# Issue order of norms, heads and weight pieces in a two-layer hybrid encoder

## The chip, the cores and the metric

The program runs on one core of a Trainium2 chip. The metric is the device time of one execution in microseconds (us), as the median of several runs. The profile is of one execution.

## The reference

Two layers of a macaron block run over one sequence of 256 tokens with 1024 channels, in float32. What matters here:

```python
def swiglu(h, w_gu, w_down):
    g, u = jnp.split(h @ w_gu, 2, axis=-1)
    return (jax.nn.silu(g) * u) @ w_down

for l in range(DEPTH):                      # DEPTH = 2, D_MODEL = 1024, D_FF = 2816
    x = x + 0.5 * swiglu(rmsnorm(x, g_ffn1[l]), w_ffn1_gu[l], w_ffn1_down[l])
    x = x + hybrid_mixer(rmsnorm(x, g_mix[l]), ...)
    x = x + 0.5 * swiglu(rmsnorm(x, g_ffn2[l]), w_ffn2_gu[l], w_ffn2_down[l])
return rmsnorm(x, g_final)
```

The mixer makes one input projection of `h` and splits its columns into three kinds of attention heads of width 64. Six forgetting heads add to the scores a running sum of log-sigmoid forget logits:

```python
c = jnp.cumsum(jax.nn.log_sigmoid(f_logit), axis=1)
bias = c[:, :, start:end, None] - c[:, :, None, :end]
p = jax.nn.softmax(jnp.where(mask, s + bias, -jnp.inf), axis=-1)
```

Five stick-breaking heads use a reversed cumulative sum of log(1 - sigmoid) in place of a softmax. Five sparse heads attend only to the 64 keys that an indexer scores highest for each query:

```python
rel = relu(einsum('bqhd,bkd->bqhk', iq, ik)); score = einsum('bqhk,bqh->bqk', rel, iw)
_, sel = lax.top_k(score, 64)
```

Each kind has its own up-projection (384, 320 and 320 rows) to 1024 channels, multiplied by a sigmoid gate (3 x 1024 gate columns of the input projection); the sum goes through one output projection.

## The kernel before

**Products.** Every weight is split into two float16 parts, `whi` and `wlo`, and the activations likewise; a projection adds three products (hi x hi, hi x lo, lo x hi) for each block of 128 rows. `project_T` (line 337) keeps the weight as the stationary operand and moves the 256 tokens; `project` (lines 372 to 374) does it the other way round.

**Weight pipeline.** All weights are cut into chunks, in the order in which they are used. `emit_raw` issues the DMA of a raw float32 part from SyncE into one of `RAW_BUFS` = 5 buffers. `emit_piece` turns a part into a piece, `whi` on ScalarE (line 249) and `wlo` on VectorE (line 251), in one of `HL_BUFS` = 6 buffer pairs. `advance(i)`, called when piece `i` is about to be used, issues pieces up to `i + HL_BUFS` and raw loads `RAW_BUFS` ahead of the last of them. Up-projections of 320 rows end in a block of 64 rows; it is loaded twice, to both halves of the partitions, is a piece of its own, and takes two products instead of three.

**Steps beside the projections.** Work that is not a projection lives in generators, the tasks. After every second block of 128 rows (every fourth where a chunk has 256 columns or less), `background()` takes one step of the first two tasks in the list. A `yield` ends a step. `finish()` takes all the remaining steps of a task at once. The tile framework then fixes an order for each engine: an instruction that is issued earlier has priority, and one that a planner's model of times holds not yet ready is passed by those behind it. On the chip each engine keeps that order.

**Norms.** `Norm.half` makes the split parts of the next activations and squares; the task `stats` then sums the squares by a product (`ss`, line 520), makes `rstd` (`power` on GpSimd), and on its last step spreads it over the partitions by a product (`rb`, line 546). `stats` has two empty steps, then `ss`, then an empty one, then `rb`. In `ffn`, `gate(k)` scales the first half of the gated unit by that result and applies SiLU; it is tried before every block of the `u` chunk, does nothing for `k < 4` while the result is missing, and from `k = 4` on takes the steps of the norm itself. `FirstNorm` does the same for the first norm of the program, from transposes of the input `x`; its squares run on ScalarE inside its `stats`.

**Mixer order.** Input groups 0 and 1 (indexer, sparse queries and latent), 2 and 3 (forgetting keys and queries), 4 (forgetting values and forget logits), 5 to 7 (stick-breaking), then six gate chunks. `indexer` is a task from group 1 on, `latent` from group 2 on, `forget` from group 5 on. `forget` makes `fr` from the logits in its first step; its second is the cumulative product `cps` (line 946) and then the operands `kb` and `qb`. The heads are tasks in pairs: three of `fox_heads`, three of `dsa_heads`, and, after group 7, three of `stick_heads`; the last of either five is a single head. A pair makes its operands, waits three steps, makes scores, and ends with `values`. The first step of `fox_heads` calls `t_f.finish()`. After the gate chunks every task left is finished at once; then come sigmoids, which are ordered behind all exponentials (line 1145), six up-projections and the output projection.

**Buffers that heads share.** PSUM tag `at` has two banks for scores and cumulative sums; tag `qT` has four buffers, one for a head's operand and two more for the split sums of a stick-breaking head; tag `mm` has four banks for projections.

Of the kernel before, what the change touches and what calls it, by code (L numbers as in the profile page):

```python
# [129 lines left out]
def trunk(ctx, tc, io, out, flag):  # L130
# [69 lines left out]
    RAW_BUFS, HL_BUFS = (4, 6) if wide else (5, 6)  # L200
    raws, pieces, chunk_pieces = [], [], []
    for ci, (nm, l, r, c, n) in enumerate(chunks):
        nk = -(-r // P)
        rk = 4 if n > 256 else 8
        pk = rk // 2 if wide else rk
        cuts = [0, 1, 2, 3, 4, 6, 8] if ci == 0 else [0, 2, 4, 6, 8] if ci == 1 else list(range(0, nk, rk)) + [nk]
        lst = []
        for k0, k1 in zip(cuts, cuts[1:]):
            ks = list(range(k0, k1))
            raws.append((ci, ks))  # L210
            full = [k for k in ks if (k + 1) * P <= r]
            for i in range(0, len(full), pk):
                sub = full[i:i + pk]
                lst.append(len(pieces))
                pieces.append((len(raws) - 1, sub[0] - k0, len(sub), P, sub))
            if len(full) < len(ks):
                k = ks[-1]
                lst.append(len(pieces))
                pieces.append((len(raws) - 1, k - k0, 1, r - k * P, [k]))
        chunk_pieces.append(lst)  # L220

# [4 lines left out]
    def emit_raw():  # L226
# [4 lines left out]
        t = wp.tile([P, RAW], F32, tag="raw", bufs=RAW_BUFS, name=f"raw{i}")  # L231
# [40 lines left out]
    def advance(i):  # L272

        while state["piece"] < min(state.get("hold", len(pieces)), i + HL_BUFS):
            emit_piece()
        last = pieces[state["piece"] - 1][0]
        while state["raw"] < min(len(raws), last + RAW_BUFS):
            emit_raw()


    class Task:
        def __init__(self, gen):
            self.gen, self.done, self.steps = gen, False, 0
            tasks.append(self)
# [20 lines left out]
    def background(n=2):  # L305
        for t in list(tasks[:n]):
            t.step()
# [7 lines left out]
    def project_T(nm, l, c, n, rhs, banks, ready=None):  # L315
# [8 lines left out]
        for pi in plist:  # L324
            advance(pi)
            wh, wl = hl_tiles[pi]
            half = pieces[pi][3] == HD
            for j, k in enumerate(pieces[pi][4]):
                if ready:
# [73 lines left out]
    nc.scalar.dma_start(grow0, io["g_ffn1"].rearrange("l (k p) -> (l k) p", p=P))  # L403
    for t in range(NT):
# [20 lines left out]
    warm_up(9)  # L425
# [53 lines left out]
    class Norm:  # L479
# [34 lines left out]
        def stats(self):  # L514
            yield
            yield
# [46 lines left out]
    class FirstNorm(Norm):  # L563


        def __init__(self, gcol, nm):
# [3 lines left out]
            self.copies, self.last = [], ()  # L570
# [19 lines left out]
        def begin(self, ks=range(4)):  # L590
# [6 lines left out]
            if k == 3:  # L597
                state["hold"] = state["piece"]
            else:
                self.task = Task(self.stats())  # L600

# [4 lines left out]
        def stats(self):  # L606
            self.ss = sp.tile([P, NT, 2], F32, tag="ss", name="ss" + self.nm)
            for h in range(2):
                for k, v in self.copies[2 * h:2 * h + 2]:
                    copy = behind(nc.scalar.copy(xT[:, k - 1:k + 1, :], v), self.last[0])  # L610
                yield
                for t in range(NT):
                    behind(square(x[:, t, h * 512:(h + 1) * 512], self.ss[:, t, h:h + 1], f"{self.nm}_{h}{t}"),
                           copy)
            yield
            ms = self.mean_square()
# [6 lines left out]
    def ffn(l, gu, dn, norm, nxt):  # L623
# [10 lines left out]
        for c, n in FF_CHUNKS:  # L634
# [5 lines left out]
            def gate(k):  # L640
                if s or (norm.R is None and k < 4):
# [121 lines left out]
    def mixer(l, norm, nxt):  # L763
# [101 lines left out]
        def indexer():  # L865
# [31 lines left out]
            for i in range(TOPK // 8):  # L897
# [4 lines left out]
                yield  # L902
            X["pen"] = sp.tile([P, 3 * P], BF16, tag="pen", name="pen" + L)
# [27 lines left out]
        def forget():  # L931
# [11 lines left out]
            yield  # L943
# [74 lines left out]
        def fox_heads(heads, nm):  # L1018
            t_f.finish()
# [4 lines left out]
            for _ in range(3):  # L1024
                yield
            kb, qb = X["kb"], X["qb"]
# [74 lines left out]
        t_idx = Task(indexer())  # L1101
        group(*IN_GROUPS[1], [(0, WC, True, PQC), (WC, P, False, PCKV)])
        t_lat = Task(latent())
# [6 lines left out]
        t_f = Task(forget())  # L1110

        for i, hs in enumerate(pairs(HA)):
            Task(later(fox_heads(hs, f"a{l}"), 2 * (i == 1)))
# [125 lines left out]
```

## Time and profile before

| | us |
|---|---|
| median of 3 runs | 1162.74 (1158.06 to 1163.47) |
| the profiled execution | 1166.04 |
| its span, first to last instruction | 1164.2 |
| TensorE busy in the span | 1126.7 |
| VectorE busy | 776.9 |
| ScalarE busy | 618.8 |
| DMA read from HBM | 207.35 MB |

The span is what the instructions take; 1.8 us of the profiled execution lie around it. Matmuls are pipelined, so a busy TensorE is not TensorE at its peak, and a stretch at half clock counts as busy too.

### The profile page before, as it was taken

The numbers are of one execution on the slowest core, as the hardware profiler recorded it, in microseconds if no ns is written. First come the engines' busy times: TensorE is split into PE (matmuls) and PEld (weight loads), VectorE is DVE, ScalarE is ACT, GpSimd is POOL, SyncE is SP. The second block draws the span as 40 slices with busy tenths as digits, with TensorE's granted clock in tenths as the row PEclk, the third lists the DMA queues.
The fourth block names the chain that finished last, engine by engine and source line by source line (L and its number), as shares of the span: only waits on it lengthen the run. The fifth ranks groups of instructions, "written<-read, shape, count | busy, mean of one in ns | idle before, by whom it ended". The sixth has DMA issues, their size and how long they took to land.

```text
span 1164.2 us, 22885 instructions
## 1 busy us (share of the span) xinstructions
PE 1126.7 (97%) x9752; PEld 964.2 (83%) x9752; DVE 776.9 (67%) x1357; ACT 618.8 (53%) x841; POOL 12.9 (1%) x25
## 2 busy tenths in 40 slices
PE   8999999989999999999999999999999999999997
PEld 7788887767888878888888888867788887888756
DVE  5865655897657966564576574579965789555642
ACT  6644544666657644353454363366575685544530
POOL 0000000000000000000000000000000000000000
PEclk9999999999999989999999999999999999999998
DMA  8956655455333866466665475556533249455711
GB/s 296 367 166 209 218 164 168 150 181 182 110 91 107 293 218 173 157 233 201 218 209 166 167 234 174 174 169 201 183 128 110 78 157 331 159 164 182 248 41 40
DMA packets 118770, 209.95 MB, mean 180 GB/s; under 512 B 4818, under 2 KB 43908, under 8 KB 118660
## 3 DMA queue, kind: packets, MB, share of 16 engines
q1 hardware_dynamic: 118340, 207.88, 54.9%
q8 instruction: 78, 1.28, 0.4%
q10 hardware_dynamic: 320, 0.53, 0.1%
q14 instruction: 32, 0.26, 0.1%
HBM read 207.35 MB, written 1.05 MB: 179 GB/s over the span
## 4 chain that ended last, share of the span: by engine, by line
PE 76%; DVE 13%; ACT 5%; issue 3%; DMA 1%; POOL 1%; POOLq 0%; DVEq 0%; ACTq 0%
PE uw_ffn_gu L337 19%; PE gw_ffn_gu L337 17%; PE d0w_ffn_down L337 7%; PE gt L337 7%; PE d512w_ffn_down L337 7%; DVE wlo L251 7%; PE in L337 3%; ACT whi L249 3%; PE up L337 1%; DMA raw<-in_w_ffn_gu_dram 1%; PE in L374 1%; PE in L372 1%; PE in L373 1%; DVE xTlof L493 1%; PE ya L974 1%
## 5 line engine op out<-in xcount | busy, mean ns | idle before, releaser
L251 DVE SCALAR_TENSOR_TENSOR wlo<-raw,whi 128x2048 f16<-128x2048 f32 (+7 forms) x232 | 452.7, 1954 | 268.4 <-ACT whi L249 267.7
L337 PEld LDWEIGHTS <-whi 128*128 128x128 f16 x5504 | 540.8, 99 | 69.9 <-issue 2.6
L249 ACT ACTIVATE whi<-raw 128x2048 f16<-128x2048 f32 (+7 forms) x232 | 379.2, 1640 | 400.6 <-issue 136.6
L337 PEld LDWEIGHTS <-wlo 128*128 128x128 f16 x2768 | 272.7, 99 | 37.5 <-issue 3.0
L337 PE MATMUL gw_ffn_gu<-xTlof,whi 128*128 128x256 f16 x704 | 194.1, 276 | 1.0 <-DVE xTlof L493 1.0
L337 PE MATMUL gw_ffn_gu<-xThif,wlo 128*128 128x256 f16 x704 | 193.9, 276 | 0.8 <-DVE wlo L251 0.8
L337 PE MATMUL gw_ffn_gu<-xThif,whi 128*128 128x256 f16 x704 | 193.9, 276 | 0.0
L337 PE MATMUL uw_ffn_gu<-xThif,whi 128*128 128x256 f16 x704 | 192.8, 274 | 0.0
L337 PE MATMUL uw_ffn_gu<-xTlof,whi 128*128 128x256 f16 x704 | 192.7, 274 | 0.0
L337 PE MATMUL uw_ffn_gu<-xThif,wlo 128*128 128x256 f16 x704 | 192.6, 274 | 0.0
L337 PE MATMUL gt<-xThimx,whi 128*128 128x256 f16 x384 | 104.8, 273 | 0.0
L337 PE MATMUL gt<-xTlomx,whi 128*128 128x256 f16 x384 | 104.7, 273 | 0.0
L337 PE MATMUL gt<-xThimx,wlo 128*128 128x256 f16 x384 | 104.7, 273 | 0.0
L337 PE MATMUL d0w_ffn_down<-ahw_ffn_gu,whi 128*128 128x256 f16 x264 | 72.0, 273 | 0.0
L337 PE MATMUL d0w_ffn_down<-ahw_ffn_gu,wlo 128*128 128x256 f16 x264 | 72.0, 273 | 0.0
L337 PE MATMUL d512w_ffn_down<-ahw_ffn_gu,whi 128*128 128x256 f16 x264 | 72.0, 273 | 0.0
L337 PE MATMUL d512w_ffn_down<-alw_ffn_gu,whi 128*128 128x256 f16 x264 | 72.0, 273 | 0.0
L337 PE MATMUL d0w_ffn_down<-alw_ffn_gu,whi 128*128 128x256 f16 x264 | 72.0, 273 | 0.0
L337 PE MATMUL d512w_ffn_down<-ahw_ffn_gu,wlo 128*128 128x256 f16 x264 | 72.0, 273 | 0.0
L337 PE MATMUL in<-xThimx,whi 128*128 128x256 f16 x176 | 49.6, 282 | 0.0
L337 PE MATMUL in<-xTlomx,whi 128*128 128x256 f16 x176 | 49.5, 281 | 0.0
L337 PE MATMUL in<-xThimx,wlo 128*128 128x256 f16 x176 | 49.4, 281 | 0.0
(326 smaller groups left out, 1374.4 us busy)
## 6 DMA issues: line engine op xcount, KB each, us to landing
raw<-in_w_ffn_gu_dram SPq DMA_DIRECT2D x60, 1024.0 KB, 5.4
raw<-in_w_ffn_down_dram SPq DMA_DIRECT2D x39, 1024.0 KB, 5.1
raw<-in_w_in_dram SPq DMA_DIRECT2D x26, 1024.0 KB, 5.0
raw<-in_w_ffn_gu_dram SPq DMA_DIRECT2D x32, 768.0 KB, 4.6
raw<-in_w_in_dram SPq DMA_DIRECT2D x12, 768.0 KB, 4.4
raw<-in_w_out_dram SPq DMA_DIRECT2D x8, 1024.0 KB, 5.0
raw<-in_w_ffn_down_dram SPq DMA_DIRECT2D x7, 512.0 KB, 3.7
raw<-in_w_in_dram SPq DMA_DIRECT2D x4, 896.0 KB, 4.7
```

The lines of the kernel that those rows point to most:

```text
L249: a = nc.scalar.activation(hv, src, AF.Copy, scale=scale)
L251: return a, nc.vector.scalar_tensor_tensor(lv, src, scale, plain(hv), op0=ALU.mult, op1=ALU.subtract, **more)
L337: m = nc.tensor.matmul(o, u, v[:, k, :], start=(k == 0 and q == 0 and b % 2 == 0), stop=(end and q == len(ops) - 1))
L372: nc.tensor.matmul(o, a, wh, start=(k == 0), stop=False)
L373: nc.tensor.matmul(o, a, wl, start=False, stop=False)
L374: state["last"] = nc.tensor.matmul(o, b, wh, start=False, stop=(k == lastk))
L493: nc.vector.scalar_tensor_tensor(self.lo[:, k, :], src, g, plain(self.hi[:, k, :]), op0=ALU.mult, op1=ALU.subtract))
L974: m = nc.tensor.matmul(o, v(h, ks), w[:, i * P:(i + 1) * P], start=(i == 0), stop=(i == 2))
```

## The change

It has these parts. (1) ScalarE's table is loaded by an instruction of its own at the start, and the first warm-up of TensorE has five products instead of nine. (2) The raw parts of the first chunk go into one tile of their own (the buffer `bigA`, which is not in use yet); there are four raw buffers instead of five, and seven pairs `whi`, `wlo` instead of six. (3) A block of 64 rows is no longer a piece of its own but is joined to the full blocks before it. (4) `stats` has three empty steps instead of two, and `gate` waits until `k = 6`. (5) `FirstNorm` makes the first half of its squares ahead of the second half of its transposes, the second half with high priority, and its copies to `xT` later. (6) `indexer`, `latent` and `forget` are side tasks: `background` steps all of these and, beside them, the first two of the others. (7) `indexer` has two yields after each of its eight top-k steps, `forget` three between `fr` and `cps`. (8) The pairs of `fox_heads` start two steps later, and `t_f.finish()` stands behind their three empty steps.

```diff
-    RAW_BUFS, HL_BUFS = (4, 6) if wide else (5, 6)
+    RAW_BUFS, HL_BUFS = (4, 6) if wide else (4, 7)
...
-            full = [k for k in ks if (k + 1) * P <= r]
-            for i in range(0, len(full), pk):
-                sub = full[i:i + pk]
+            for i in range(0, len(ks), pk):
+                sub = ks[i:i + pk]
                 lst.append(len(pieces))
-                pieces.append((len(raws) - 1, sub[0] - k0, len(sub), P, sub))
-            if len(full) < len(ks):
-                k = ks[-1]
-                lst.append(len(pieces))
-                pieces.append((len(raws) - 1, k - k0, 1, r - k * P, [k]))
+                pieces.append((len(raws) - 1, i, len(sub), r // P if r % P else None, sub))
...
-        t = wp.tile([P, RAW], F32, tag="raw", bufs=RAW_BUFS, name=f"raw{i}")
+        if ci == 0:
+            if i == 0:
+                raw_tiles["first"] = sp.tile([P, D // P, n], F32, tag="bigA", name="raw_first")
+            t = raw_tiles["first"].rearrange("p k n -> p (k n)")[:, ks[0] * n:]
+        else:
+            t = wp.tile([P, RAW], F32, tag="raw", bufs=RAW_BUFS, name=f"raw{i}")
...
-        while state["raw"] < min(len(raws), last + RAW_BUFS):
+        while state["raw"] < min(len(raws), max(last, cuts0 - 1) + RAW_BUFS):
...
-        for t in list(tasks[:n]):
+        for t in [t for t in tasks if t.side] + [t for t in tasks if not t.side][:n]:
             t.step()
...
+    table0 = nc.scalar.preload_act_table_set("natural_log_exp_and_others")
...
-    warm_up(9)
+    warm_up(5)
...
@@ class Norm @@
         def stats(self):
-            yield
-            yield
+            for _ in range(3):
+                yield
...
@@ class FirstNorm, begin @@
             if k == 3:
+                self.squares(0)
                 state["hold"] = state["piece"]
             else:
+                self.last = self.copy(0), self.last[1]
                 self.task = Task(self.stats())
+
+        def squares(self, h):
+            for t in range(NT):
+                i = behind(square(x[:, t, h * 512:(h + 1) * 512], self.ss[:, t, h:h + 1], f"{self.nm}_{h}{t}"),
+                           self.last[0])
+                self.last = i, self.last[1]
+
+        def copy(self, h):
+            for k, v in self.copies[2 * h:2 * h + 2]:
+                i = behind(nc.scalar.copy(xT[:, k - 1:k + 1, :], v), self.last[0])
+            return i
...
         def stats(self):
-            for h in range(2):
-                for k, v in self.copies[2 * h:2 * h + 2]:
-                    copy = behind(nc.scalar.copy(xT[:, k - 1:k + 1, :], v), self.last[0])
-                yield
-                for t in range(NT):
-                    behind(square(x[:, t, h * 512:(h + 1) * 512], self.ss[:, t, h:h + 1], f"{self.nm}_{h}{t}"),
-                           copy)
-            yield
+            yield
+            with tc.high_priority():
+                self.squares(1)
+            yield
+            self.copy(1)
...
-                if s or (norm.R is None and k < 4):
+                if s or (norm.R is None and k < 6):
...
@@ indexer, after each top-k step @@
                 yield
+                yield
...
@@ forget, between fr and cps @@
-            yield
+            for _ in range(3):
+                yield
...
         def fox_heads(heads, nm):
-            t_f.finish()
...
             for _ in range(3):
                 yield
+            t_f.finish()
...
-        t_idx = Task(indexer())
+        t_idx = Task(indexer(), True)
...
-        t_lat = Task(latent())
+        t_lat = Task(latent(), True)
...
-        t_f = Task(forget())
+        t_f = Task(forget(), True)
...
-            Task(later(fox_heads(hs, f"a{l}"), 2 * (i == 1)))
+            Task(later(fox_heads(hs, f"a{l}"), 2 + 2 * (i == 1)))
```

## Rows read from the trace of the kernel before

**Rows 1.** The page: TensorE's busy time; its granted clock in 40 slices.

```profile
PE 1126.7 (97%) x9752; PEld 964.2 (83%) x9752; DVE 776.9 (67%) x1357; ACT 618.8 (53%) x841; POOL 12.9 (1%) x25
...
PEclk9999999999999989999999999999999999999998
```

**Rows 2.** TensorE's waits: waiter, releaser, us in total, times, longest.

```profile
PE ssf L520 <- DVE accf L509: 4.1, 3, 1.9
PE cps L946 <- issue: 3.7, 1, 3.7
PE cps L946 <- DVE fr L941: 3.6, 1, 3.6
PE rbf L546 <- DVE dgf L542: 2.9, 1, 2.9
...
PE up L337 <- DVE gt L1157: 1.0, 2, 0.5
```

**Rows 3.** Stretches: length; busy us (x) of PE, PEld, DVE, ACT, POOL; clock; DMA.

```profile
28.53:31.46 2.93, 0.00 (x1) 0.03 (x1) 2.03 (x8) 2.45 (x2) 0.71 (x1) 1.00 1.05 391
31.78:35.19 3.41, 3.41 (x17) 2.20 (x16) 3.41 (x3) 2.87 (x3) 0.00 (x0) 0.50 1.06 392
242.33:246.03 3.70, 0.00 (x2) 0.03 (x1) 3.62 (x9) 2.27 (x4) 0.00 (x0) 1.00 0.73 269
412.04:413.97 1.93, 0.00 (x1) 0.00 (x1) 1.93 (x4) 0.14 (x1) 0.00 (x0) 1.00 0.53 201
414.08:420.89 6.81, 6.81 (x33) 5.28 (x34) 2.83 (x7) 0.11 (x1) 0.69 (x1) 0.50 0.88 308
344.80:366.60 21.80, 21.31 (x187) 18.32 (x185) 14.19 (x29) 14.51 (x27) 0.00 (x0) 1.00 0.28 98
220.00:270.00 50.00, 46.19 (x369) 36.40 (x368) 48.79 (x137) 32.28 (x60) 0.00 (x0) 0.97 0.55 184
```

**Rows 4.** TensorE in order of time, the first nine microseconds.

```profile
1.82 4.21 PE L423 MATMUL warm<-ident 128*128 128x128 f32 x18 [1.82 <-POOL ident masks.py:199]
...
7.92 1.06 PE L423 MATMUL warm<-ident 128*128 128x128 f32 x8
8.88 0.28 PE L337 MATMUL gw_ffn_gu<-xThif,whi 128*128 128x256 f16 x1
```

**Rows 5.** ScalarE in order of time, its first two instructions.

```profile
6.54 1.28 ACT L492 ACT_TABLE_LOAD   x1 [6.54 <-DVE gT L416]
7.83 0.47 ACT L492 ACTIVATE xThif<-xpf,gT 128x256 f16<-128x256 f32 x1
```

**Rows 6.** ScalarE, the last square of the first norm.

```profile
27.71 0.61 ACT L477 ACTIVATE sqf<-x 128x512 f32<-128x512 f32 x1
```

**Rows 7.** Products of one tile in a stretch: group 5; second norm's chunk; up-projections.

```profile
237.20:242.33 5.13, 5.13 (x47) 1.00 0.71 215
...
403.90:412.00 8.10, 8.10 (x72) 1.00 1.01 362
...
355.80:366.60 10.80, 7.22 (x60) 1.00 0.27 102
```

**Rows 8.** VectorE in order of time, what `cps` and `ss` waited for.

```profile
245.65 0.27 DVE L941 COPY fr<-f 128x36 f32<-128x36 f32 x2
...
413.23 0.68 DVE L509 TENSOR_TENSOR accf<-accf,sqf 128x512 f32<-128x512 f32 x1
```

**Rows 9.** ScalarE at the end of the first layer's heads.

```profile
352.54 0.41 ACT L818 ACTIVATE Tb<-pr 64x256 fp32r<-64x256 f32 x1 [1.45 <-PE cb L1081]
...
363.93 1.28 ACT L1145 ACT_TABLE_LOAD   x1
```

**Rows 10.** VectorE, one pass over a stick-breaking head's sums.

```profile
359.62 0.56 DVE L1072 SCALAR_TENSOR_TENSOR lb<-sb,eb 128x384 f32<-128x384 f32 x1
```

**Rows 11.** VectorE's weight parts by shape: count, busy us, mean ns.

```profile
L251 DVE SCALAR_TENSOR_TENSOR wlo<-raw,whi 128x1536 f16<-128x1536 f32 x50 | 87.8, 1756 | 63.2 <-ACT whi L249 63.2
...
L251 DVE SCALAR_TENSOR_TENSOR wlo<-raw,whi 128x512 f16<-128x512 f32 x12 | 8.2, 687 | 4.8 <-ACT whi L249 4.7
```

More of the change, by code (lines that the diff above doesn't have):

```diff
@@ L210, in trunk @@
             raws.append((ci, ks))
-            full = [k for k in ks if (k + 1) * P <= r]
-            for i in range(0, len(full), pk):
-                sub = full[i:i + pk]
+            for i in range(0, len(ks), pk):
+                sub = ks[i:i + pk]
                 lst.append(len(pieces))
-                pieces.append((len(raws) - 1, sub[0] - k0, len(sub), P, sub))
-            if len(full) < len(ks):
-                k = ks[-1]
-                lst.append(len(pieces))
-                pieces.append((len(raws) - 1, k - k0, 1, r - k * P, [k]))
+                pieces.append((len(raws) - 1, i, len(sub), r // P if r % P else None, sub))
         chunk_pieces.append(lst)
+        if ci == 0:
+            cuts0 = len(raws)
     raw_dma = []
@@ L230, in emit_raw @@
         src = io[nm][l]
-        t = wp.tile([P, RAW], F32, tag="raw", bufs=RAW_BUFS, name=f"raw{i}")
+        if ci == 0:
+            if i == 0:
[3 more added lines that the diff above has]
+            t = wp.tile([P, RAW], F32, tag="raw", bufs=RAW_BUFS, name=f"raw{i}")
         t = t[:, :len(ks) * n].rearrange("p (k n) -> p k n", n=n)
@@ L276, in advance, with __init__ @@
         last = pieces[state["piece"] - 1][0]
-        while state["raw"] < min(len(raws), last + RAW_BUFS):
+        while state["raw"] < min(len(raws), max(last, cuts0 - 1) + RAW_BUFS):
             emit_raw()
     class Task:
-        def __init__(self, gen):
-            self.gen, self.done, self.steps = gen, False, 0
+        def __init__(self, gen, side=False):
+            self.gen, self.done, self.steps, self.side = gen, False, 0, side
             tasks.append(self)
@@ L326, in project_T @@
             wh, wl = hl_tiles[pi]
-            half = pieces[pi][3] == HD
             for j, k in enumerate(pieces[pi][4]):
+                half = k == pieces[pi][3]
                 if ready:
@@ L569, in __init__ @@
             self.ps = {}
-            self.copies, self.last = [], ()
+            self.copies, self.last = [], (table0,)
+            self.ss = sp.tile([P, NT, 2], F32, tag="ss", name="ss" + self.nm)
         def block(self, k):
@@ L606, in stats @@
         def stats(self):
-            self.ss = sp.tile([P, NT, 2], F32, tag="ss", name="ss" + self.nm)
-            for h in range(2):
-                for k, v in self.copies[2 * h:2 * h + 2]:
-                    copy = behind(nc.scalar.copy(xT[:, k - 1:k + 1, :], v), self.last[0])
-                yield
-                for t in range(NT):
-                    behind(square(x[:, t, h * 512:(h + 1) * 512], self.ss[:, t, h:h + 1], f"{self.nm}_{h}{t}"),
-                           copy)
             yield
+            with tc.high_priority():
+                self.squares(1)
+            yield
+            self.copy(1)
             ms = self.mean_square()
```

## The prediction

> **What bounds the kernel now.** I read the page first, then TensorE's waits, then the busy time by stretch, last the order in time around each wait. TensorE is busy for 97% of the span [rows 1], so only its idle time, its slow time and its instruction count can move the end. The change adds and removes no projection product; it drops eight warm-up instructions. The waits should be read for what is long: four rows hold 14.3 us [rows 2]: `ssf` (the sum of squares of the norm behind a mixer, once per layer; the third of its times is short), `cps` (the forget gates' cumulative product, once per layer) and `rbf` (the first norm). The granted clock tells the rest: after each of these gaps it stands at 0.50, that is 1.2 instead of 2.4 GHz, for 3.41 us behind the 2.93 us gap and for 6.81 us behind the 1.93 us gap [rows 3]. Such a stretch counts as busy but does half its work, so it costs half its length, 1.7 or 3.4 us. Behind the `cps` gap I take 1.7. The clock line of the page shows the places again only faintly [rows 1], so the stretches have to be cut at the gaps to see them.
>
> **The norm behind the mixer (part 4).** A step falls due after 24 products of a `gw` chunk. 72 products took 8.10 us and the gap begins right there [rows 3, 7], so `ss` stood where it was issued, behind the third step, and 24 products are 2.7 us. It waited 1.93 us for the last addition on VectorE [rows 8]. One empty step more puts it 2.7 us later, 0.8 us more than it needs. Gain per layer 1.93 + 3.4 = 5.3 us, for two layers 10.7; nothing, if VectorE comes as much later as TensorE comes earlier. `rb` moves by a step as well and keeps its distance of 48 products (5.4 us) from `ss`. `gate` then runs at k = 4 instead of 2; half of the `u` chunk, 48 products, still hides the multiplication and SiLU. Cost nothing; without that cover about a step, 2.7 us.
>
> **The first norm (part 5).** `rb` came 2.93 us late; the last square on ScalarE ended at 28.32 [rows 6], 3.1 us before `rb` started at 31.46 [rows 3]. The squares now stand ahead of the weight parts that were in their way, and the data are in SBUF early. They have to move by 2.93 us; I take all of the gap and its slow stretch, 2.93 + 1.7 = 4.6 us. Lower bound nothing.
>
> **The forget gates (parts 6 to 8).** Before, the first pair's `finish()` issued `cps` in the same call as `fr`. 47 products of group 5 [rows 7] had run before the gap, so the planner had already put it back from product 18. Now it is issued behind the fourth step, that is behind all 72 products: 25 more at 5.13/47 us are 2.7 us. If `fr` came no earlier, 3.70 - 2.7 = 1.0 us of the gap would be left. But `fr` comes earlier: the pair's operands stand two steps behind the logits instead of ahead on ScalarE, and with the doubled yields three of the eight top-k steps are issued behind `fr` instead of before it, on a VectorE that is busy 48.79 of 50 us there [rows 3]. I take the whole gap and half of the slow 3.41 us: 5.4 us a layer, 10.75 for both; bounds 8.8 (1.0 left in each) and 10.75. What is late next: `kb`, `qb` and the pair's scores, two steps behind `cps`, on that same VectorE. If the stall only moves there, the 10.75 come back. For this and for short waits in the pairs, below, I take off 3 us, bounds 0 and 10.75.
>
> **Start (part 1).** The table load took 1.28 us between the gains and the first split part [rows 5], and nine warm-up products took 4.21 us in 18 instructions [rows 4], so four fewer are 1.9 us. But the second warm-up ran until 8.98, into the first product at 8.88 [rows 4], at the faster of two rates (8 in 1.06 us against 18 in 4.21), and weights must arrive too. I take 0.7 us, between nothing and 1.28, as the load's own length is all that the chain surely loses. For the lower end: if the clock comes later for lack of warm-up by as much as the longest slow stretch, 6.81 us, it costs 3.4 us. The Trainium skill (ScalarE: Activation LUTs, What ACT_TABLE_LOAD costs) adds a drain to each load, 2.66 us in all; the next instruction here starts 0.01 us behind the load [rows 5], so the trace does not agree, and by the page the sum would be up to 1.4 us better. The Trainium skill (TensorE: Matmul & The Clock Gate, What's actually happening) says that the slow clock is the default and activity lifts it; that speaks against a shorter warm-up, the two rates of the warm-up agree with it, and by it the sum would be up to 3.4 us worse.
>
> **Buffers and pieces (parts 2 and 3).** No weight part is among the long waits of TensorE [rows 2], so an earlier part ends nothing: 0. Eight pieces fewer save VectorE at most 8 x 0.687 = 5.5 us [rows 11], hidden behind TensorE. SyncE's queue issues the same loads in the same order, those of the first chunk without waiting for a buffer; four raw buffers and seven pairs look as far ahead as five and six. If that cover were gone, each late part would show as a wait on `wlo`; I keep 0.
>
> **The end of the heads (parts 6 and 8).** From group 5 to the last gate chunk there are 4 + 2 + 4 + 24 = 34 calls, each with two steps for the head tasks: 68. Before, the pairs needed 71 steps and `forget` one: 4 were left, the last single head from its scores on. Now they need 77, as each fox pair starts two later: 9 are left, the values of two pairs and the last head from its operands on. Pairs now also run in lockstep: third fox with first sparse, second with third sparse, first with second stick. TensorE has 60 up-projection products to cover the end [rows 7]; then it needs gates, whose sigmoids stand behind the last exponential. That chain took 352.54 to 363.93, 11.4 us, from the last head's operand to the table load for the sigmoids [rows 9], and left a wait of 0.5 us per layer at `up` [rows 2]. Attention products that come behind the gate loop let the loop end earlier by their own time, so TensorE reaches the point where it must wait no later; the question is when VectorE and ScalarE are done. In the last 21.8 us it was busy for 14.19, idle 7.6 [rows 3]. Into this come two more heads of four passes at 0.56 [rows 10], 4.5 us, and up to three joined parts of 1.756 for ones of 0.687 [rows 11], 3.2: together 7.7 us, as much as all its idle time, in a chain that alternates with ScalarE. I take 3 us of delay and, since that gap is of the size that lowered the clock, 2.2 us for it (between 1.7 and 3.4): 5.2 a layer, 10.4 for both. Bounds: 0, and the whole chain in the open with the longer slow stretch, 11.4 + 3.4 = 14.8 a layer.
>
> **Sum.** Gains 10.7 + 4.6 + 10.75 + 0.7 = 26.75; costs 10.4 + 3 = 13.4; net -13.4. The profiled execution took 1166.0 (span 1164.2), so it would take 1152.6; it lies 3.3 above the median of the runs, 1162.7, which becomes 1149.3.
>
> **Rivals.**
> *Nothing takes the place of the gaps.* VectorE's idle 7.6 us [rows 3] hold the added 7.7, or the planner fills the end. 1162.7 - 26.75 = 1136.0; with small leftovers 1136 to 1143. Against it: pairs in lockstep share two banks `at` and four buffers `qT`.
> *The stall of the forget gates moves.* VectorE has no room in 220:270 [rows 3]; the scores take over the whole gap and slow clock, and the end costs its 10.4: -26.75 + 10.4 + 10.75 = -5.6, 1157.1, and worse with the 3 us of short waits: 1160.
> *The steps do not move what they name.* The planner puts products where it holds them ready (`cps` stood 29 products behind its place of issue [rows 7]); then only the start and the first norm count: 1162.7 - 5.3 = 1157.4. Against it: `ss` stood exactly at its place.
> *Slower: the last head's chain runs alone.* The one place is the end of the gate loop. If the chain starts only there and two weight parts of 1.756 get in, a layer loses 11.4 + 3.4 + 3.5 = 18.3; twice this less 26.75 is +9.9, 1172.6. It decides from 13.4 us a layer on. For it: no step of the last head comes before the loop's end. Against it: the operands of the last head need only buffers that the pairs ahead give back, and 60 products plus those of three pairs still lie beside the chain.
>
> **How the numbers follow.** My forecast, 1143 to 1155 as its own range: 0.47. Nothing in their place: 0.24. Moved stall: 0.13. Steps without effect: 0.06. Slower: 0.10. A measurement of this kernel can tell about 0.5%, 5.8 us. Faster by more than that: the first two and 0.02 of the moved stall, 0.73. Within: 0.17. Slower: 0.10. The range leaves out the best third of the second case and the slower one: 1138 to 1163.
>
> **What would show it.** Right: no wait of `ssf`, `cps` and `rbf` over 1 us and full clock around 30, 245 and 412 us; ScalarE's table load first of all; a wait at `up` of 2 to 5 us with a stretch at 0.50 behind it in each layer. Wrong: a wait at `sa` behind `kb` and `qb` of the length of the old one; a wait of `ssf` that stays; a wait at `up` over 13 us; or weight parts as releasers of TensorE.

## The result and the profile after

The changed kernel takes 1174.8 us (median of 4 runs, 1174.17 to 1176.59) against 1163.1 us of the kernel before beside it: a ratio of 1.0107, interval 1.0068 to 1.0145. It is slower; the prediction was 13 us faster. The profiled execution of after took 1174.17 us, its span is 1172.4. So the two spans differ by 8.2 us and the medians by 11.7: the profiled execution of before lies about 3 us above the median of its runs, that of after at the low end of its own. The runs of before beside the experiments spread from 1157.96 us at a mean granted clock of 0.995 to 1166.37 us at 0.986, and the profiled one stands at 0.987.

TensorE's part of the page, as in [rows 1]; the busy time is the same, so all of the longer span is idle time of TensorE, and the clock line shows three faint places instead of one in its middle:

```profile
PE 1126.7 (96%) x9744; PEld 962.4 (82%) x9744; DVE 776.4 (66%) x1341; ACT 617.2 (53%) x833; POOL 12.9 (1%) x25
...
PEclk9999999999998999999999999999899989999999
```

TensorE's waits of after, as in [rows 2]. `ssf` and `rbf` are gone from the list, as predicted; at its head stands a wait that the prediction named as the sign of being wrong, the scores `sa` for `qb`. Below it is a group that the list of before does not have: sums and values of the stick-breaking heads, `cb` and `yb`, and a longer `up`.

```profile
PE sa L151 <- DVE qb L977: 7.8, 2, 3.9
PE yb L989 <- ACT eb L787: 2.9, 4, 1.2
PE up L339 <- DVE gt L1172: 2.5, 2, 1.3
PE cb L1096 <- ACT hb L476: 2.4, 2, 1.2
...
PE up L339 <- DVE y L253: 1.6, 2, 0.8
```

Where did the time go? Cut both spans where TensorE begins the next kind of product. The stretches of before, in this order: gate and up products of the first feed-forward; the mixer's input groups; its gate loop; its up-projections; gate and up products of the second feed-forward; the same product kinds of layer 2's second feed-forward; and what lies behind the last product (columns as in [rows 3]):

```profile
8.88:131.74 122.86, 119.14 (x1069) 105.12 (x1069) 85.37 (x128) 72.51 (x79) 0.71 (x1) 0.99 0.76 256
189.38:268.79 79.41, 72.93 (x553) 54.83 (x551) 72.16 (x189) 49.79 (x95) 3.52 (x3) 0.98 0.56 178
268.79:357.79 89.00, 87.44 (x776) 75.47 (x774) 56.30 (x116) 56.82 (x121) 0.00 (x0) 1.00 0.37 115
357.79:382.03 24.24, 23.71 (x213) 20.52 (x211) 20.67 (x39) 21.61 (x29) 0.00 (x0) 1.00 0.37 119
403.89:526.04 122.15, 120.22 (x1069) 106.45 (x1067) 78.28 (x106) 57.64 (x54) 0.69 (x1) 0.97 0.62 201
...
973.60:1097.74 124.14, 122.00 (x1084) 108.21 (x1082) 78.86 (x109) 59.78 (x58) 0.69 (x1) 0.97 0.61 198
1155.57:1164.17 8.60, 0.00 (x1) 0.00 (x0) 1.88 (x6) 0.72 (x1) 0.55 (x1) 0.65 0.20 70
```

The same stretches of after, and the up-projections of layer 2 (925.36:964.54):

```profile
7.04:126.78 119.74, 117.55 (x1069) 104.28 (x1067) 87.17 (x132) 73.47 (x80) 0.71 (x1) 1.00 0.79 268
184.42:261.94 77.52, 70.43 (x530) 53.29 (x528) 70.19 (x181) 46.97 (x85) 3.55 (x3) 0.98 0.57 177
261.94:349.58 87.64, 84.88 (x754) 72.32 (x752) 53.86 (x109) 54.32 (x117) 0.00 (x0) 1.00 0.45 145
349.58:388.23 38.65, 33.70 (x257) 27.39 (x255) 29.28 (x52) 28.32 (x40) 0.00 (x0) 0.91 0.26 84
409.76:526.29 116.53, 116.53 (x1069) 104.43 (x1067) 73.78 (x104) 56.64 (x54) 0.69 (x1) 1.00 0.61 195
...
925.36:964.54 39.18, 33.99 (x257) 27.40 (x255) 29.28 (x52) 28.32 (x40) 0.00 (x0) 0.91 0.27 83
986.07:1104.34 118.27, 118.27 (x1084) 106.21 (x1082) 74.16 (x107) 58.68 (x58) 0.69 (x1) 1.00 0.60 192
1162.17:1172.39 10.22, 0.01 (x1) 0.00 (x0) 1.88 (x6) 0.72 (x1) 0.55 (x1) 0.72 0.17 59
```

In these two executions the norms pay what they should: the first product starts 1.84 us earlier, the first feed-forward is 3.1 us shorter, and the two second feed-forwards are 5.6 and 5.9 us shorter, at full clock and without any idle time. All of it is lost in the up-projections: 38.65 and 39.18 us instead of 24.24. They hold 257 products instead of 213. The input groups and the gate loop hold 45 fewer, but became only 1.9 and 1.4 us shorter. Another 1.6 us lie behind the last product.

### The profile page after: what moved, and what is told of

Read it like the earlier page. It is cut to its first block, busy times and chain, and to the rows that moved or that the text cites. A ratio compares the mean times of both kernels' runs of the same rounds, so it can differ in the third digit from the quotient of the medians.

```text
span 1172.4 us, 22850 instructions
## 1 busy us (share of the span) xinstructions
PE 1126.7 (96%) x9744; PEld 962.4 (82%) x9744; DVE 776.4 (66%) x1341; ACT 617.2 (53%) x833; POOL 12.9 (1%) x25
## 3 DMA queue, kind: packets, MB, share of 16 engines
HBM read 207.35 MB, written 1.05 MB: 178 GB/s over the span
## 5 line engine op out<-in xcount | busy, mean ns | idle before, releaser
L253 DVE SCALAR_TENSOR_TENSOR wlo<-raw,whi 128x2048 f16<-128x2048 f32 (+5 forms) x218 | 446.6, 2050 | 254.7 <-ACT whi L251 254.5
L251 ACT ACTIVATE whi<-raw 128x2048 f16<-128x2048 f32 (+5 forms) x218 | 374.0, 1718 | 409.1 <-issue 95.7
L339 PEld LDWEIGHTS <-wlo 128*128 128x128 f16 x2768 | 271.6, 98 | 38.7 <-issue 4.8
L339 PE MATMUL gw_ffn_gu<-xTlof,whi 128*128 128x256 f16 x704 | 191.7, 273 | 0.8 <-DVE xTlof L496 0.8
L339 PE MATMUL gw_ffn_gu<-xThif,wlo 128*128 128x256 f16 x704 | 191.5, 273 | 1.0 <-DVE wlo L253 0.9
L339 PE MATMUL up<-y,whi 128*128 128x256 f16 x256 | 48.6, 285 | 4.1 <-DVE gt L1172 2.5
```

What stands on the lines that cost most here:

```text
L251: a = nc.scalar.activation(hv, src, AF.Copy, scale=scale)
L253: return a, nc.vector.scalar_tensor_tensor(lv, src, scale, plain(hv), op0=ALU.mult, op1=ALU.subtract, **more)
L339: m = nc.tensor.matmul(o, u, v[:, k, :], start=(k == 0 and q == 0 and b % 2 == 0), stop=(end and q == len(ops) - 1))
```

## Experiments

Twelve kernels ran. Each was timed in turn with the kernel before, on the same chip, in three rounds or five; its own median stands first, then its ratio to before, with a 95% interval. The kernel before had medians of 1161.1 to 1163.1 us beside them and beside the changed kernel, so that medians of different runs can be compared to about 2 us. The theory after reading the two profiles: the order of the mixer's steps (parts 6 to 8) makes the loss, at the end of the heads and at `sa`. The rival: the buffers and the larger pieces (parts 2 and 3) make it, since weight parts of 2.28 us stand between the heads' operations on VectorE.

**1. The mixer's steps undone (parts 6 to 8).**

```diff
-        for t in [t for t in tasks if t.side] + [t for t in tasks if not t.side][:n]:
+        for t in list(tasks[:n]):
...
-            Task(later(fox_heads(hs, f"a{l}"), 2 + 2 * (i == 1)))
+            Task(later(fox_heads(hs, f"a{l}"), 2 * (i == 1)))
```

(and one yield again in `indexer` and `forget`, `t_f.finish()` first in `fox_heads`.)

> The changed kernel with the order of steps in the mixer as before (parts 6 to 8 undone: first two tasks of the list, one yield after a top-k step, one in forget, fox heads not later, finish of forget first). Theory S (the order of steps makes the end of the heads late): the losses of about 13 us per mixer go, the gaps of the first norm and of the norm behind the mixer stay away, the gap at cps of 3.7 us comes back: 1147 us, ratio 0.986. Theory B (joined pieces and seven pairs put longer weight parts in front of the last head): the end stays late, 1158 or more, ratio 0.995 or more.

1154.2 us, 0.9925 (0.9901 to 0.9949). The up-projections are back at 24.45 us, and so is the wait of `cps`, 3.2 us a layer. So parts 6 to 8 cost 20.6 us (1174.8 less 1154.2): the theory holds against the rival. It is 7 us more than the expected 1147; experiments 6 and 11 show where 4 of them are.

**2. The mixer's steps alone**, parts 6 to 8 in the kernel before.

> The kernel before with parts 6 to 8 alone. Theory S: 10.8 + 12.7 us more than before, 1186 us, ratio 1.020, with waits of about 5 us in sum at the end of each mixer's heads. Theory B: with the old buffers and pieces the end costs little, 1160 to 1170, ratio below 1.006.

1178.6 us, 1.013 (1.0105 to 1.0155), and up-projections of 37.75 us. The loss needs none of the other parts; `sa` waits 4.0 us a layer here too. It is less than the theory's sum, 1186, and the trace shows why: the wait of `ssf` behind the mixer, 4.1 us before, and the slow stretch behind it are nearly gone here, though `stats` is the old one; why the sums come in time there stays open. The first layer's second feed-forward:

```profile
PE ssf L520 <- DVE accf L509: 1.4, 3, 1.1
...
416.65:533.62 116.97, 116.79 (x1068) 104.42 (x1066) 76.28 (x104) 57.72 (x54) 0.69 (x1) 1.00 0.61 203
```

It is 5.2 us shorter than before, that of layer 2 4.5 us; the output projections behind the late heads are 3.1 and 0.7 us longer. So most of what part 4 gains came here without it, and the gain of part 4 and the cost of parts 6 to 8 cannot be added up as if they were independent.

**3. The two later steps of the fox pairs undone**, everything else of the change left in.

```diff
-            Task(later(fox_heads(hs, f"a{l}"), 2 + 2 * (i == 1)))
+            Task(later(fox_heads(hs, f"a{l}"), 2 * (i == 1)))
```

> The changed kernel, but the fox pairs start two steps earlier, as before; all else as changed. Pairs no longer run in lockstep and the last single head has its operands before the loop ends. Theory S, with the two later steps as the part that does it: the end is as before, 1150 to 1155, ratio 0.99. Theory S with the side tasks as the part, or theory B: above 1168.

1154.7 us, 0.9927 (0.9901 to 0.9953). The waits at `sa` and `cps`, and the up-projections:

```profile
PE sa L151 <- DVE qb L977: 6.6, 2, 3.3
...
PE cps L961 <- issue: 1.3, 1, 1.3
...
353.84:379.21 25.37, 23.93 (x212) 20.54 (x210) 22.06 (x34) 21.94 (x27) 0.00 (x0) 1.00 0.39 128
```

This one line is worth 20.1 of the 20.6 us. What is left of parts 6 to 8, the stepping beside the heads and the later `cps`, is worth 0.5 us, that is nothing: the wait of `cps` fell from 3.2 us (experiment 1) to 1.3, and `sa` now waits 3.3 us for `qb`.

**4. Three heads' tasks in each step beside the gate chunks**, the pairs still two steps later.

```diff
-                background()
+                background(beside)      # 3 in the gate chunks, 2 elsewhere
```

> The changed kernel, but beside the gate chunks three head tasks take a step at each call instead of two, so that all heads end before the loop does. Theory S: no wait at the end, 1174.8 less 2 x 11 to 13, 1149 to 1153, ratio 0.99. Rival (the two score banks and four operand buffers are the limit, not the steps): three tasks at once wait for each other, 1165 or more.

1157.6 us, 0.9952 (0.9936 to 0.9968), between the expected 1149 to 1153 and the rival's 1165. The up-projections:

```profile
358.82:380.76 21.94, 21.94 (x203) 19.50 (x201) 19.15 (x28) 15.60 (x15) 0.00 (x0) 1.00 0.46 162
```

They take 21.94 us with 203 products and no idle time, less than before, and the gate loop 95.3 us, as 56 products moved into it (810 against 754). Input groups, gate loop and up-projections of layer 1 together take 195.6 us, against 203.8 in the changed kernel and 193.5 in experiment 3. So the loss at the end is what the lateness leaves behind the loop; with the same lateness and all heads inside the loop it is gone. What stays are waits of 3.9 us at `sa` and 1.4 us at `o` a layer.

**5. The norm behind the mixer alone (part 4)** in the kernel before.

```diff
-            yield
-            yield
+            for _ in range(3):
+                yield
...
-                if s or (norm.R is None and k < 4):
+                if s or (norm.R is None and k < 6):
```

> The kernel before with the later norm statistics alone (one empty step more in the norm behind a mixer, the gate's bound 6 instead of 4). If the gain that the changed kernel shows at this place stands by itself (the time from the first product of the second feed-forward to its down projection fell by 5.6 and 5.9 us there), the time falls by 11 to 12 us, to 1151 to 1152 us, no wait at the sum of squares stays, and nothing else moves. The rival: the gain is only there because the mixer's end comes otherwise in the changed kernel; then the time falls by less than 5 us, to over 1158 us.

1154.2 us, 0.9941 (0.9924 to 0.9958), before 1161.4 beside it. The wait of `ss` is gone and the profiled feed-forwards are 5.5 and 5.6 us shorter, but the timed gain is 7.2 us, between the expected 11 to 12 and the rival's 5: the span of before, against which the larger number is read, is that of an execution of 1166.04 us, 4.6 above the median beside these runs. Part 4 gains without any change to the mixer; that a changed mixer takes most of the same gain without part 4 is what experiment 2 shows.

**6. Buffers and pieces undone (parts 2 and 3).**

```diff
-    RAW_BUFS, HL_BUFS = (4, 6) if wide else (4, 7)
+    RAW_BUFS, HL_BUFS = (4, 6) if wide else (5, 6)
```

(and the 64-row pieces and the first chunk's raw buffers as before.)

> The changed kernel with five raw and six part buffers, 64-row pieces by themselves and the first chunk in raw buffers again (parts 2 and 3 undone). If buffers and pieces play no part in the loss, the time is that of the changed kernel within 0.3%, 1171 to 1178 us, and the end of the heads in each layer stays 14 us longer than before. If the joined parts of 2.28 us that stand in VectorE's queue between the last heads' operations make the loss, the time falls by their difference of about 1.1 us for each of three and by the slow stretches behind it, to 1160 to 1168 us. If the time behind the last product, 1.6 us longer in the changed kernel, comes from these parts, it goes back to 8.6 us here.

1170.6 us, 1.0077 (1.0053 to 1.0101); up-projections 37.65 us. It fell between what the two sides said: parts 2 and 3 cost 4.2 us, but only 0.9 of it at the end of the heads, up-projections and output projections of both layers taken together (120.9 us in after, 120.0 here). 1.6 us of it are the time behind the last product, which is 8.6 us here. The transfers of the stretch behind the last product differ in the queue of instructions; first after, then this kernel (queue, kind, packets, MB, share):

```profile
q14 instruction: 8, 0.07, 1.8%
```

```profile
q14 instruction: 7, 0.06, 2.2%
```

The output lands in 3.6 to 3.8 us from its issue in both; after fetches one more packet of instructions there. That holds for every kernel here: 8 packets and 10.2 to 10.4 us in the changed one and in experiments 1, 3, 4 and 7 to 10, which have the new buffers and pieces; 7 packets and 8.6 us in the one before and in 2, 5, 6, 11 and 12, which have the old ones. In the records of after, SyncE's closing instructions stand still from 1169.40 to 1170.99, and two packets of instructions begin at 1169.34 and 1169.41; before and experiment 6 have no gap like it. That the fetch makes the gap fits, but no run shows it apart from the buffers and pieces.

**7. The forget gates' operations on VectorE put ahead**, on top of experiment 3.

```diff
-            nc.vector.tensor_copy(c1, cps[:NB, :SEQ])
...
+            with tc.high_priority():
+                nc.vector.tensor_copy(c1, cps[:NB, :SEQ])
...
```

> The changed kernel with the fox pairs started as before, and with VectorE's operations of the forget gates (up to the logits' sums, and from the cumulative product to the bias rows of the keys and queries) put ahead of other ready work in the planner. With the pairs started as before alone it took 1154.7 us and still waited 1.3 us a layer at the cumulative product and 3.3 us at the first scores. If those waits come from other work that stands between these operations on VectorE (a weight part of 2.28 us, sums, maxima), they fall to under 1.5 us together and the time to 1145 to 1150 us. The rival: the chain of a dozen operations is itself longer than the products beside it, or what is pushed behind is late in its turn; then the time stays at 1153 us or more.

1155.3 us, 0.9946 (0.9926 to 0.9967): no change against experiment 3. A weight part of 2.29 us still stood in the chain, and the waits stayed 1.3 us at `cps` and 3.4 us at `sa`. The rival holds: priority in the planner does not shorten this chain.

**8. The first fox pair two steps later than before, and so together with the second.** In the kernel of experiment 7:

```diff
-            Task(later(fox_heads(hs, f"a{l}"), 2 * (i == 1)))
+            Task(later(fox_heads(hs, f"a{l}"), 2 * (i < 2)))
```

> The same with the first fox pair alone started two steps later (so that it runs in lockstep with the second); by the count of steps 6 are left behind the gate loop, all of the last head, against 4 with the pairs started as before and 9 in the changed kernel. If the loss at the end of the heads follows the number of steps left, it lies between: up projections of 28 to 32 us a layer against 25.4 and 38.7, so 5 to 12 us more than with the pairs started as before, 1152 to 1160 us. If only lockstep of the last pairs counts, the end of the heads is as with the pairs started as before, and the time 1145 to 1150 us.

1161.0 us, 1.0 (0.9991 to 1.001), 5.8 us more than experiment 7. The size came out as expected and the place did not. Its input groups, gate loop and up-projections:

```profile
184.69:261.54 76.85, 69.12 (x529) 52.07 (x527) 69.83 (x181) 46.87 (x85) 3.55 (x3) 1.00 0.55 175
261.54:356.59 95.05, 91.53 (x799) 77.35 (x797) 61.13 (x125) 60.53 (x131) 0.00 (x0) 1.00 0.42 136
356.59:381.96 25.37, 23.93 (x212) 20.52 (x210) 22.11 (x34) 21.94 (x27) 0.00 (x0) 1.00 0.40 127
```

The up-projections are those of experiment 3, with 212 products: nothing more is left behind the loop, though by the count of steps six should be, against four there. The loop itself has 3.5 us of idle time (95.05 less 91.53). TensorE's waits name what lockstep costs:

```profile
PE sa L861 <- ACT pa L787: 4.5, 4, 2.1
PE sa L151 <- DVE qb L979: 3.7, 2, 1.9
```

The scores of one pair wait for the exponentials of the other to read a score bank, 2.1 us a layer that is not among the long waits of experiment 7.

**9. The third fox pair started as before**, the first two as in the changed kernel.

```diff
-            Task(later(fox_heads(hs, f"a{l}"), 2 + 2 * (i == 1)))
+            Task(later(fox_heads(hs, f"a{l}"), 2 * (i < 2) + 2 * (i == 1)))
```

> The changed kernel with its third fox pair alone started as before (the first two stay two steps later). By the count of steps 7 are left behind the gate loop, one of them the values of the second stick pair, against 6 where nothing was lost at the end (up projections of 25.4 us) and 9 in the changed kernel (38.7). If the loss begins where values of a pair and the whole last head come to stand behind the gate loop, up projections take 30 us or more a layer and the time is 1165 to 1172 us; if it takes two pairs' values there, they take 25 to 28 us and the time is 1158 to 1163 us.

1170.7 us, 1.0077 (1.005 to 1.0103). Its up-projections:

```profile
353.54:386.90 33.36, 28.12 (x230) 23.56 (x228) 24.86 (x42) 23.62 (x32) 0.00 (x0) 0.90 0.32 97
```

33.4 us and 230 products: between 25.4 with 212 and 38.7 with 257, as the first of the two cases said. The values of one pair and the whole last head behind the loop are enough for most of the loss.

**10. Six buffers for the heads' operands instead of four** in the changed kernel (a fallback path that does not run here gives up a part buffer to make the room).

```diff
-            T = sp.tile([P, 512], F32R, tag="qT", bufs=4, name="T" + nm)
+            T = sp.tile([P, 512], F32R, tag="qT", bufs=6, name="T" + nm)
```

> The changed kernel with six buffers for the heads' operands (qT) instead of four, nothing else. In the changed kernel the last head's operand T is begun 10.3 us behind the gate loop, when the cumulative sums of the pair ahead have given their buffers back. If the loss at the end of the heads is the wait for these buffers, the operand moves ahead to within 4 us of the gate loop's end, the up projections fall from 38.7 and 39.2 us to 30 us or less, and the time to 1155 to 1163 us. If the last pairs are simply late (their work comes behind the gate loop with weight parts and each other on VectorE and ScalarE), the up projections stay at 35 us or more and the time at 1168 us or more.

1170.0 us, 1.0068 (1.0051 to 1.0085); up-projections 37.37 us. The last head's operand was begun 6.3 us behind the gate loop instead of 10.3, and the table load only 2.4 us earlier, counted the same way. The time is 4.8 us below that of the changed kernel: the buffers are a part of the delay, not the cause.

**11. Parts 1, 4 and 5 alone**: the mixer's steps, buffers and pieces of before (the edits of experiments 1 and 6 together).

> Parts 1, 4 and 5 alone: the start, the first norm and the later norm statistics, with the mixer's steps and the buffers and pieces of the kernel before. With the mixer's steps undone but the new buffers and pieces kept it took 1154.2 us, spent 10.4 us behind the last product and 89.8 us in each gate loop; with the buffers undone too these go back to 8.6 us and 89.0 us if they belong to parts 2 and 3. Then the time is 1154.2 less 1.8 and 1.6, 1150 to 1152 us. The rival: the start needs the new buffers (the first chunk's parts without waiting for a raw buffer), so the early norm comes late again; then 1154 us or more.

1150.2 us in five rounds, 0.9895 (0.9876 to 0.9914). The gate loop is 89.0 us and the end 8.6 us again. So of the whole, 1162.8 us beside these runs: parts 1, 4 and 5 save 12.6 us, parts 2 and 3 cost 4.0 (experiment 1 less this one), parts 6 to 8 cost 20.6. The sum is 12.0 us more, 1174.8; it has to be, as the three are steps of one way from before to the changed kernel. Taken in another order they differ: put on the kernel before, parts 6 to 8 cost 16.0 (experiment 2).

**12. The first two fox pairs one step later, not two; the third not at all**, with buffers and pieces of before.

```diff
-            Task(later(fox_heads(hs, f"a{l}"), 2 + 2 * (i == 1)))
+            Task(later(fox_heads(hs, f"a{l}"), (i < 2) + 2 * (i == 1)))
```

> Parts 1, 4, 5 and the stepping beside the heads, with the first two fox pairs one step later than before instead of two, the third not at all, and the buffers and pieces of before. By the count of steps 5 are left behind the gate loop, and the pairs do not run in lockstep. If what the loss needs is lateness of the last pairs by more than that, and the stall at the first scores shrinks by a step of 24 products, 2.7 us, then up projections take 24 to 26 us a layer, the waits at the cumulative product and the scores fall from 4.7 to about 2 us a layer, and the time is 1145 to 1150 us. If every step of delay costs at the end of the heads, up projections take 28 us or more and the time is 1152 us or more.

1147.1 us in five rounds, 0.9876 (0.9855 to 0.9896), the lowest median of all. The up-projections take 24.23 us. The expected relief at `sa` did not come: the wait is 3.7 us a layer, in place of the one at `cps`, which is down to 0.8. Against experiment 11 it is 3.1 us. The profiles put that into the input groups of layer 2, 76.6 us against 80.5, where experiment 11 has 6.83 us at half clock at `cps` and this kernel, at a wait as long, 3.7 us, none; what makes the difference stays open.

## Why the prediction was wrong

**Start, first norm, norm behind the mixer: right in the mechanism, 3.4 us too large in the sum.** Predicted -16.0 us, read in the spans -1.8, -3.1 and -11.5, timed -12.6 (experiment 11). The term that was mis-sized is "Gain per layer 1.93 + 3.4 = 5.3 us": it was read from one execution of before, with the longer slow stretch in both layers, and alone it timed 7.2 us for both and not 10.7 (experiment 5). The first norm gave 3.1 us instead of 4.6: a wait of 1.2 us for `s0w` follows in the same feed-forward. In experiment 11, without parts 2 and 3, that wait is not there, and the first feed-forward's gate and up products end 6.2 us earlier than before, where 5.3 were predicted for start and norm. The cost of up to 3.4 us for a shorter warm-up did not come: the first feed-forward of after stands at 1.00 from its first product on, 7.04 us. The Trainium skill (TensorE: Matmul & The Clock Gate, What's actually happening) says that the slow clock is the default and activity lifts it. The rates of after agree with that: 10 warm-up instructions in 2.50 us at first, and the later 8 in 1.06 us.

**The forget gates: the step that failed is "I take the whole gap".** It set 10.75 us for `cps` and took off 3 for what is late next. The wait of `cps` did fall to 0.57 us, but nothing was gained, as the rival "the stall of the forget gates moves" came in full: experiment 3 has all of this part without the later pairs, and at 1154.7 us is not faster than experiment 1 with 1154.2, which has none of it. VectorE of after in order of time shows why:

```profile
242.46 2.29 DVE L253 SCALAR_TENSOR_TENSOR wlo<-raw,whi 128x2048 f16<-128x2048 f32 x1
...
245.54 0.41 DVE L966 CAST c<-cps 128x256 bf16<-128x256 f32 x1
...
248.11 2.28 DVE L253 SCALAR_TENSOR_TENSOR wlo<-raw,whi 128x2048 f16<-128x2048 f32 x1
...
251.31 1.61 DVE L977 TENSOR_SCALAR qb<-c,c_fsel 128x256 bf16<-128x256 bf16 x6
```

And TensorE at the same time:

```profile
240.88 1.10 PE L961 MATMUL cps<-c_tri,fr 128*128 128x256 f32 x4 [0.57 <-issue]
...
251.70 0.43 PE L151 MATMUL sa<-kb,qb 128*128 128x128 bf16 x2 [3.88 <-DVE qb L977]
```

From the end of `cps`, 241.98, to the scores that need `qb`, 251.70, are 9.7 us, nearly half of it two weight parts of 2.3 us. The two steps between `cps` and these scores, of 24 products or 2.7 us each [rows 7], and the first products of the scores cover 5.8 of it, and 3.9 stay open. Before, `cps` was issued by the pair's first step, three ahead of its scores, and no wait of `sa` was long. A later `cps` moves the whole chain, and the wait with it. The prediction knew that VectorE had no room there [rows 3] and gave the case 0.13.

**The end of the heads: the right place, half the size.** The step that failed is "I take 3 us of delay". The term was 5.2 us a layer, with 2.2 of slow clock in it. It measured 20.1 us for two layers (experiment 3 against the change), 10 a layer. The delay that was put at 3 us can be read on ScalarE of after, beside [rows 9]:

```profile
359.89 0.41 ACT L831 ACTIVATE Tb<-pr 64x256 fp32r<-64x256 f32 x1
...
368.08 0.52 ACT L787 ACTIVATE eb<-eb 128x384 f32<-128x384 f32 x1 [1.94 <-DVE eb L1099]
368.62 1.28 ACT L1160 ACT_TABLE_LOAD   x1
```

Counted from the first gate product, the last head's operand came 83.8 us later before (352.54 less 268.79) and 98.0 now (359.89 less 261.94): 14.2 us of lateness. The chain behind it shrank from 11.4 to 8.7 us, so the table load is 11.5 us late, not 3. The prediction compared amounts of work with idle time on VectorE; it should have asked when the chain can begin. The 10 us lie midway between the value that it took and its upper bound, 14.8. The sums of two pairs stand ahead of the last head on both engines, with two weight parts of 2.28 us among them (the prediction counted 1.756 for one), and TensorE runs out of products:

```profile
352.19 2.28 DVE L253 SCALAR_TENSOR_TENSOR wlo<-raw,whi 128x2048 f16<-128x2048 f32 x1
...
358.96 2.28 DVE L253 SCALAR_TENSOR_TENSOR wlo<-raw,whi 128x2048 f16<-128x2048 f32 x1
```

```profile
361.65 0.27 PE L339 MATMUL up<-y,whi 128*128 128x256 f16 x1 [0.80 <-DVE y L253]
...
366.19 0.45 PE L1096 MATMUL cb<-hb,negur 128*128 128x384 f32 x1 [1.20 <-ACT hb L476]
...
368.65 1.54 PE L989 MATMUL yb<-eb,pr 128*64 128x128 f32 x6 [1.20 <-ACT eb L787]
371.32 0.58 PE L339 MATMUL up<-y,whi 128*128 128x256 f16 x2 [1.12 <-DVE gt L1172]
```

Four waits in series, none over 1.2 us, make 4.3 us, and the clock falls during the third, at 367.86. So no wait of "2 to 5 us at `up`" appeared: the reader who looks for one long wait misses it. Over input groups, gate loop and up-projections of layer 1 together, 203.8 us instead of 192.7, TensorE has 6.2 us more idle time (14.8 against 8.6) and 4.9 us more busy time (189.0 against 184.1) for the same products. The slow clock is 3.4 of the 4.9, half of 10.24 us against half of 3.41; the other 1.5 is not placed. Up to the last product the two executions have the same 23.9 us at half clock: the change moved the slow stretches and did not add to them.

**The slower rival was the one that came, in its place and not in its size.** It said 18.3 us a layer against gains of 26.75, 1172.6 us; what came is 10 a layer and 4.0 for the buffers against gains of 12.6. That its time lies 2 us from the measured one is luck: its loss of 36.6 us was 24.6, and its gain of 26.75 was 12.6. Its condition, that the last head's chain starts only at the end of the gate loop, held and more: the operand `Tb` is begun 10.3 us behind the loop in the changed kernel. In experiment 9, with the values of one pair still to come, it is 1.7 us behind, and the up-projections take 33.4 us; in experiment 8 it lies 6.3 us ahead of the loop's end, 356.59, and they take 25.4:

```profile
350.33 0.41 ACT L831 ACTIVATE Tb<-pr 64x256 fp32r<-64x256 f32 x1 [0.18 <-PE cb L1098]
```

What decided was the lateness of the pairs ahead of the last head, which set when its chain can begin. The chain itself took 8.7 us and not the 11.4 + 3.5 of the rival, and products lay beside it.

**Buffers and pieces: the step "I keep 0" failed by 4.0 us.** About 1.6 are the end of the program, 0.8 a layer the gate loop (89.8 against 89.0 us in experiments 1 and 11). A third place is the first feed-forward: its gate and up products end between 126.8 and 128.3 us in the eight kernels with the new buffers and pieces, which all wait 1.0 to 2.7 us for `s0w` there, and between 125.3 and 126.2 in experiments 6, 11 and 12, with parts 1 and 5 but the old ones, where that wait is 0.7 us or not in the list. What makes the gate loop longer stays open: no wait of TensorE in it was over 0.6 us in either.

Together: 13.4 us faster was predicted and 11.7 slower came, 25 apart. 3.4 of it are the size of the norms and the start, 8.3 the forget gates (7.75 predicted, 0.5 lost), 9.7 the end of the heads (10.4 predicted, 20.1 lost), 4.0 the buffers and pieces.

## What to carry to other kernels

A step that delays one task by two slots delays everything that queues for its slot, down to the last head; count what then lies behind the loop in products and in the moment at which the last chain can begin, not in idle time of an engine. Moving a product later ends its own wait but carries the whole chain behind it: add up that chain, weight parts included, before a gain is booked. Where several parts are changed at once, undo them in groups, and in more than one order, as two parts can take the same gain: here 12.6 us of gain were hidden under 24.6 of loss. Parts 1, 4 and 5 alone are 1.05% faster than before, a version with one step instead of two and the old buffers 1.2%. And a gain that is read from one profiled execution holds for that execution; its slow stretches need not be in the others.

## What the runs showed of the hardware

The granted clock fell after some waits and not after others of the same length. In after it stood at 0.50 in these four stretches, behind `sa` and behind the series of waits of about 1.2 us at the end of the heads, in both layers:

```profile
251.80:255.21 3.41, 3.41 (x18) 2.49 (x18) 3.37 (x14) 1.14 (x3) 0.00 (x0) 0.50 0.82 293
367.86:374.69 6.83, 4.91 (x23) 3.56 (x24) 3.22 (x7) 6.58 (x12) 0.00 (x0) 0.50 0.01 2
825.25:832.08 6.83, 5.74 (x26) 3.88 (x27) 6.76 (x22) 2.16 (x7) 0.00 (x0) 0.50 0.48 154
944.70:951.53 6.83, 5.48 (x27) 3.81 (x26) 4.08 (x8) 6.82 (x13) 0.00 (x0) 0.50 0.00 0
```

The same wait of 3.9 us brought 3.41 us at half clock in one layer and 6.83 in the other. In experiment 8 waits of 1.9 and 2.1 us a few microseconds apart brought none: its three stretches above stand at 1.00. In experiment 3 the wait of 3.3 us at `sa` brought 3.41 us at half clock in layer 2 and none in layer 1; in experiment 12 that of 3.7 us brought 6.83 us in layer 1 and none in layer 2. Before, 1.93 us were enough [rows 3].

And the end of the span was 1.6 us longer wherever one more packet of instructions was fetched behind the last product (10.2 to 10.4 us against 8.6); that the fetch is the cause is not shown.
